# A hybrid decoder layer: the low parts of 20 weight blocks and the decay masks computed by VectorE, the last output group in halves, and a new instruction order

## The chip, the cores and the metric

The kernel runs on one core of a Trainium2 chip. The metric is the device time of one execution in microseconds (us); where several executions are given, their median. The engines are named as the profile names them: PE is the matrix engine (TensorE) and PEld its weight loads, DVE is VectorE, ACT is ScalarE, POOL is GpSimd, SP is SyncE, which in this kernel only issues DMAs. Each engine works through its own instructions in program order and waits on semaphores for the others.

## The reference

One decoder layer on a sequence of 1024 positions with a width of 1024, all in float32. The input is normalised and modulated by a vector `c`, projected to 3080 columns, and goes through two mixers: a gated linear recurrence (LRU, 4 blocks of 128 channels) and a gated delta rule in chunks (GDN, 4 heads of 128). An output projection, a residual and a squared-ReLU MLP with 4096 hidden columns follow.

```python
h = rms_norm(x, norm_mix_w[l]) * (1.0 + sc1) + sh1
proj = h @ w_in[l]
...
qkv = jax.nn.silu(causal_depthwise_conv(proj[..., o_q:o_v_end], gdn_conv_w[l]))
...
# in the delta rule, per chunk (g is summed along the chunk):
decay = jnp.exp(jnp.where(causal, g[..., :, None] - g[..., None, :], -jnp.inf))
Lmat = jnp.where(strict, jnp.einsum('bhnid,bhnjd->bhnij', k_beta, k) * decay, 0.0)
tmat = Lmat + jnp.eye(C, dtype=jnp.float32)
u = lax.linalg.triangular_solve(tmat, v_beta, left_side=True, lower=True, unit_diagonal=True)
...
attn = jnp.where(causal, jnp.einsum('bhnid,bhnjd->bhnij', q, k) * decay, 0.0)
...
mix = jnp.concatenate([out_lru, out_gdn], axis=-1) @ w_out[l]
x = x + g1 * mix
h = rms_norm(x, norm_mlp_w[l]) * (1.0 + sc2) + sh2
x = x + g2 * (jnp.square(jax.nn.relu(h @ w_up[l])) @ w_down[l])
return rms_norm(x, final_norm_w)
```

## The kernel before

**Products in split precision.** The large matrix products are made with a fast matmul type of reduced precision (`fp32r`). Each operand is split into a high part, which is the value rounded to that type, and a low part, which is what the rounding left out; a product is three matmuls (high x high, high x low, low x high). So each weight block needs a high part (a copy by ACT) and a low part. For the 20 projection blocks of 128 columns that are not keys (`z`, `q`, `v` of four heads, `lx` and `ly` of four blocks) the method `split` of `Proj` (L817) makes the low part in two steps: ACT writes the negated high part into `w_l` (L821), and a DMA on POOL's queue adds the raw weights to it while it writes (L822; the helper `Adder`, L553, gives the DMA the option to accumulate). Each such block is then used by 72 matmuls of 342 columns, in three thirds of the sequence.

**The stages.** First `x` is loaded, normalised, transposed and split, and the key projections run as their data arrive. Then follow the gate columns (`ab`), from which the cumulated decays `gcs` come; they are transposed and written to a small array in DRAM, `gdr`, so that a row of it can be spread over all partitions. For each of four heads `decay` (L1081) makes the mask of 128 x 1024: SP fills `dm` with `neg` (0 on and above the diagonal of each 128 x 128 block, -1e30 below), a DMA on POOL's queue adds the broadcast row of `gdr` to it, and ACT takes the exponential in eight pieces, with the negated decay of the row as bias. `key` (L1102) multiplies the key products `kk` by the mask into `LT`. After the fourth head `inverse` (L1135) inverts all triangular blocks: a substitution of 62 short DVE instructions for blocks of 32, then many small matmuls (`it`, `iy`, `iw`, `iz`). Beside this run the projections `z`, `q`, `v`, `lx`, `ly`, and behind them the chain of the delta rule (`ch`, `cho`) and the LRU. The output projection (`wg`, `wl`), the second norm (`h2`), and the MLP follow; the MLP's two products are made with Strassen's scheme of seven block products each (`up`: `upx`, `upy`, `upz`; down: `dn`).

**The end.** The seven block products of the down projection are summed in PSUM banks. In the last one (`at == 4`) the four output groups `j` are finished one after another, each with 24 matmuls of 512 columns, and each followed by `final_late` (L1739): gate, residual, sum of squares, the power -0.5 on POOL, the scaling by ACT and DVE in halves, and the store.

**What sets the order.** The program is not issued as it is written. `Recorder` notes each operation with its engine, its buffers and a length (L239, `Proxy.length` L496); `schedule` (L291) then simulates all engines with these lengths, with latencies between engines, a model of the matrix engine's clock (`Clock`, L201) and of the port that DVE and POOL share, and takes at each step the ready operation of the highest priority. A priority comes from the latest start that the end allows, moved by a number for each operation from the table `SHIFTS` (L246), which is packed into the source as text. The main sequence of large products keeps its written order on PE; other PE operations are put between them. Operations in a group of small matmuls (`mms`) have the lengths `L1_DUR` and `L2_DUR` and a share of activity for the clock model (L1168, L1176, L1187, L1191). The result is one fixed order for each engine and one fixed placing of buffers. All recorded operations are issued from one line, 458, so the profile shows them under L458 (small groups under L636) and they are told apart by their tiles.

Of the kernel before, what the change touches and what calls it, by code (L numbers as in the profile page):

```python
# [13 lines left out]
F32 = mybir.dt.float32  # L14
# [8 lines left out]
P = 128  # L23
# [24 lines left out]
FILL, WARM, AB_DUR, GATE_DUR, L1_DUR, L2_DUR = 1e6, 36, 0.85, 0.89, 0.066, 0.11  # L48
# [5 lines left out]
T_INIT, SP_ISSUE, SP_LAT, SP_LAND, LANES = 0.75, 0.45, 1.6, 1.0, 8  # L54
RESERVE = {"b": 11, "ps": 2, "u": 1, "c": 2}
# [67 lines left out]
def dram_box(ap):  # L123
# [7 lines left out]
    'c-p;NXLuFW+Fg523J^*Fkw{enNbe{hpdd<9svy|#N)fDx6csKYQj{W15Cpv_AVsAJ77(O}6hS)DTOb04KoU|<+3Q;;&-e4r`JTy-Z}O1jWM<Fa``znZY'  # L131
    'rT7hQlTPPg9Rv$k|{^fz*)i`=+4Dl!Z*0rEHkZn%wEQJ+{QZn{yxSrIhYb$7knRcL)G{}aCab<Q}LAXu_h{*6QNa1$a*2oa4bjI#$1^7V%FOk<1@S6c{'
    'Ka!>@is-a&oigWSz-Q&-pWVQ(l9>wY<1M_0Yj!1>Zk`k3)~yF6k=?++piG<LsW)XE4a_<o@ezna2^K(YG^$v-zU=nOC?P_0hmK&FY8`@jk|+OiR6C8>A'
    '0+sv-N<5FSkFf)O^3y)yprS+f&Y@NZK-d%1ZR-!eU_q-lW4xeJ_O&NVaK>6q6dYJPMrv~wPcS?mAMc?(B4FMU7uuthK?YKIeNYUK^G^-&b_@OMrf-#T+'
    'cF&KqhzK9t-mOIQ;3v~*XFz1ko;Vg!(T*~sMv}wabEMr=j8GMl=@jQy-3YVBD&8=K^s(*b(fJscwYKI~CgNeE8oPXtBW*r3B&%EHDfVmipuD%UOF_+Op'
    'tFz3vh>6a-ScW;iCrqpvYszb6M}19vKj3lyea=Om_wVulWR3)WG;{F~m-y4nYbfuF@xA5ja>m;BXvK`&L^B$R&Kf3~@!VjJn{mPG<}d#Q7UQX4W7I<xJ'
    'cSCuXf(+FDOk%+=V&goNyxO5SvB-guxg-hC<=S+4f7Z$+cw<8ZoxdX*QZbX_pv4iVLoSvz{l|n%5y6oRLdq<%NLky9<>>v4?@?1lNlE*%+vf%t6T(C`4'
    'Ml0e#@@S#`Xs5A=U2ADdm3^2W>5szyULqt#BIW%yj&LF?hr_x4YTV#KY(83k>1b&~iI2>-DrZLuJ#8-|3zakM7wY2fqtE!4a7?*f)46l$d$luCZOR?(p'
    'GUla?7=7ixF=Uw9<<01GiEm=fB@5Ffn#y6uP#IU6`ExG!+ZpPc>ctq%TWd9|~5220u`J{7DPIGeq|Hp+P~EAGzoIsLMi=9S4v;?3Z#+y4r+$xaP4$-6&'
    'rJ9Iv0h23G7*^8RlpIi|9jMo0n<^GRs4Lj2g3iY;qb;jHAuICoZt=AUsdG6x@{C^*>*z%bFf6i=OC=nmqiNUhUv`2U}G%r*OEzyUKur3(GVfZN+3I*)J'  # L140
    'U|0KDXsNwm?!y<MGWZ>jb7QD0hTC}M^vl5>!DL%kcWcF6xDf1S8?h|T@w#2aE}>Sop?Kg+KBkqah1s|O2QY2zc|L%Jh&PSU0820lwJ``g%nsWb)wvgIb'
    '4%N1JnFxiX@X<3yJv6m3u&S8f#}@lf_?4rP>3I}rr&afKK*R71MdXZ=j_j&mBZXVtQJ@q*u(pSD??TMPXy2Ko$Sm0l&tzW0iMV{mwh@=FSj~A45bGC3S'
    'J3#jcQ(SVK6tih~F?4+w%tax7cv5R<`fuX6J3str7Ufza>~PnCGvAQAlH!9cx>oJ7)7HH!^{L*-rL0#@kz=6lGCm<)&XhcLu9rH}6F;%(I{HTics)_%|'
    '~(!vUUgwv;z*ede$iOQS2|Fr8aD0hv4#tf8pX4VDVt9ZU$s1~*^;&oL*oPaKiXmzlyH7>^d%0E(~b;s^f9=R%jPVH>UXM0`hb4F=;`Byl@htMw}NFv;`'
    'yYGMkj!}8yJ*LfSYu!xt<;!u5i)PKz1Kd?J6E?@(*1M>q@IFbA95uW6e?624iL0i7X<Lrjf%oeU*;|a@9hJDpuW=Ce5h3t)ioN7-9xp`8QSMq1Ii7B=i'
    '%jsOYc>)376;lZ>Iw5XwTH_LXiA_sKU1S<3N7uo2Ucr}94@IqzQd;TEK3+2KMHh-)$z&!+E%a51=@eZ&x>eMECYUFq?u+UYz20}-SI@U6>K9*ObC)mRv'
    '=E1v#wzovNpqU`YB~LJN~$>%tGP=$pUN5LL-VH@jNZsG4=NIa%s|9RaR%Wb#r_ra#}q6yBYc;AUpc!`C8`~k*fUtcvmEWjI?a4>Sj-Z5++5}v+mVNDNp'
    '!|E?qDi!+uCLtcPf(x;fBydej$7w$1NJ(hqlVDakiq<!uO-Eoo_jedBJzy@w1O{eD#IXQYII_@&sF%M{&{a!y~9~p22eI+7|qV%eEA{;TJs5F8CBvQPT'
# [78 lines left out]
class Recorder:  # L227
# [63 lines left out]
    def schedule(self):  # L291
# [37 lines left out]
        while done < len(ops):  # L329
# [68 lines left out]
            if e == "SP":  # L398
# [1482 lines left out]
```

## Time and profile before

| | us |
|---|---|
| median of 3 runs | 1159.14 |
| lowest, highest run | 1156.08, 1170.63 |
| the profiled execution, device time | 1170.07 |
| its span, first to last instruction | 1168.3 |
| PE busy in the span | 1145.5 |
| DVE busy | 800.1 |
| ACT busy | 630.6 |
| POOL busy | 288.1 |

The profile is of one execution, and its 1170.07 us are near the highest of the runs shown. Busy times are sums over the span; the ends of matmuls are modelled, so a busy PE is not PE at its peak. "Idle before, releaser" tells what ended an engine's idle time. A row of a stage gives its start and end, its length, the busy time and the number of instructions of PE, PEld, DVE, ACT and POOL, the clock granted to PE (1.00 is full speed), the busy share of the DMA engines, and GB/s.

### The profile page before, as it was taken

Reading aid. Unit: us, or ns where it says so; the run is one execution under the profiler, and the core shown is the slowest. Engines: PE = TensorE matmul, PEld = TensorE weight load, DVE = VectorE, ACT = ScalarE, POOL = GpSimd, SP = SyncE. Lnnn points to the kernel's source line nnn. Section 1 sums busy time; section 2 is a strip of 40 time slices with the busy share of each in tenths; the row PEclk is TensorE's granted clock in tenths of the full one; section 3 lists DMA queues with packets and bytes.
Section 4 is the critical chain, followed back from the end, with each engine's and each line's share of the span. In section 5 each row is a group of like instructions: output and inputs, shape, how many; then the busy total and the mean of one; then the engine's idle time right before and its main releaser. Section 6 shows DMA issues by size and latency. Waiting matters only on the chain.

```text
span 1168.3 us, 16601 instructions
## 1 busy us (share of the span) xinstructions
PE 1145.5 (98%) x6264; PEld 978.9 (84%) x6264; DVE 800.1 (68%) x1114; ACT 630.6 (54%) x979; POOL 288.1 (25%) x185
## 2 busy tenths in 40 slices
PE   8999799999999999999999999999999999999997
PEld 5889798999999987778888888888788888888885
DVE  3568577578885778678867777866786386774673
ACT  4736634355548988376755555455755234442541
POOL 1103110012211433200002302331115177722140
PEclk9999898799999999999999999999999999999999
DMA  9428974366775562413187776687999976776342
GB/s 344 165 70 238 306 218 145 89 195 184 234 207 165 145 236 88 144 73 109 54 282 249 269 229 224 243 283 244 357 405 348 342 263 206 252 242 208 126 172 80
DMA packets 133298, 246.35 MB, mean 211 GB/s; under 512 B 11169, under 2 KB 54366, under 8 KB 133218
## 3 DMA queue, kind: packets, MB, share of 16 engines
q1 hardware_dynamic: 129762, 232.71, 57.8%
q0 software_dynamic: 3456, 12.58, 5.8%
q8 instruction: 49, 0.80, 0.3%
q14 instruction: 31, 0.25, 0.1%
HBM read 173.93 MB, written 58.74 MB: 199 GB/s over the span
## 4 chain that ended last, share of the span: by engine, by line
PE 91%; ACT 3%; DMA 2%; issue 2%; POOL 1%; DVE 1%; SPq 0%; POOLq 0%; ACTq 0%
PE dn L458 26%; PE upx L458 15%; PE upz L458 8%; PE q_p L458 4%; PE k_p L458 4%; PE v_p L458 4%; PE upy L458 4%; PE wl L458 4%; PE lx_p L458 3%; PE ly_p L458 3%; PE z_p L458 3%; PE wg L458 2%; PE ch L458 2%; DMA k_dm<-gdr 1%; PE cho L458 1%
## 5 line engine op out<-in xcount | busy, mean ns | idle before, releaser
L458 PE MATMUL upx<-h2h,U 128*128 128x512 f32 x512 | 168.0, 394 | 0.0
L458 POOL TENSOR_TENSOR wd<-wd,wd 128x512 f32<-128x512 f32 x32 | 52.4, 1639 | 286.8 <-DMA wd<-in_w_down_dram 176.7
L458 PEld LDWEIGHTS upx<-h2h,U 128*128 128x128 f32 x512 | 96.1, 188 | 22.8 <-issue 0.2
L458 DVE TENSOR_TENSOR U<-wu,U 128x512 fp32r<-128x512 f32 x112 | 86.7, 783 | 35.1 <-ACT U L458 34.4
L458 PE MATMUL upx<-h2l,U 128*128 128x512 f32 x256 | 100.9, 394 | 0.0
L458 ACT ACTIVATE act<-act 128x512 f32<-128x512 f32 x112 | 69.5, 631 | 39.6 <-DVE act L458 37.5
L458 PE MATMUL upz<-h2h,U 128*128 128x512 f32 x256 | 84.9, 394 | 0.0
L458 ACT CAST U<-wu 128x512 fp32r<-128x512 f32 x112 | 67.0, 616 | 26.5 <-DVE wu L458 8.4
L458 PEld LDWEIGHTS upx<-h2l,U 128*128 128x128 f32 x256 | 48.1, 188 | 11.3
L458 PEld LDWEIGHTS upz<-h2h,U 128*128 128x128 f32 x256 | 48.1, 188 | 11.3
L458 PE MATMUL upz<-h2l,U 128*128 128x512 f32 x128 | 50.4, 394 | 0.0
L458 ACT COPY ek<-upx 128x512 f32<-128x512 f32 x48 | 28.1, 585 | 36.0 <-PE upx L458 35.8
L458 DVE TENSOR_TENSOR act<-upz,ek 128x512 f32<-128x512 f32 x32 | 21.9, 688 | 34.0 <-PE upz L458 30.3
L458 PE MATMUL upy<-h2h,U 128*128 128x512 f32 x128 | 42.6, 394 | 0.0
L458 DVE TENSOR_TENSOR wu<-wu,wu 128x512 f32<-128x512 f32 x48 | 39.6, 839 | 0.6 <-DMA wu<-in_w_up_dram 0.5
L458 ACT ACTIVATE vn<-ch,bcoef 128x128 f32<-128x128 f32 x32 | 11.7, 367 | 39.8 <-PE ch L458 39.6
L458 PE MATMUL q_p<-hl,q_wh 128*128 128x342 f32 x96 | 33.0, 344 | 0.0
L458 PE MATMUL q_p<-hh,q_wh 128*128 128x342 f32 x96 | 32.8, 342 | 0.0
L458 PE MATMUL q_p<-hh,q_wl 128*128 128x342 f32 x96 | 32.4, 338 | 0.0
L458 POOL TENSOR_TENSOR ssq<-ssq,mhalf 128x1 f32<-128x1 f32 x16 | 12.1, 759 | 82.0 <-DVE ssq L458 81.9
L458 PE MATMUL z_p<-hh,z_wh 128*128 128x342 f32 x96 | 31.8, 331 | 0.0
L458 PE MATMUL v_p<-hh,v_wl 128*128 128x342 f32 x96 | 31.7, 331 | 0.0
(582 smaller groups left out, 3620.8 us busy)
## 6 DMA issues: line engine op xcount, KB each, us to landing
L<-aod SPq DMA_DIRECT2D x56, 512.0 KB, 6.4
R<-in_w_down_dram SPq DMA_DIRECT2D x40, 512.0 KB, 4.8
wu<-in_w_up_dram SPq DMA_DIRECT2D x32, 512.0 KB, 6.4
aod<-as SPq DMA_DIRECT2D x64, 256.0 KB, 3.8
wd<-in_w_down_dram SPq DMA_DIRECT2D x32, 512.0 KB
aod<-act SPq DMA_DIRECT2D x48, 256.0 KB, 2.8
x<-in_x_dram SPq DMA_DIRECT2D x16, 512.0 KB, 5.7
sc_w<-in_w_mod_dram SPq DMA_DIRECT2D x16, 512.0 KB, 5.5
```

Source lines behind the costliest of these rows:

```text
L458: op.fn(*[res(v) for v in op.a], **{n: res(v) for n, v in op.k.items()})
```

## The change

- `split`: the low part is one DVE subtraction, raw weights minus high part. ACT's negated copy and the accumulating DMA are gone, in all 20 blocks.
- `decay`: SP loads the broadcast row of `gdr` straight into `dm`, and DVE adds `neg` to it. The fill with `neg` by SP and the accumulating DMA on POOL are gone, in all four heads.
- The last output group (`at == 4`, `j == 3`) is made in two halves of 256 columns: the first half in its old PSUM bank, the second in a bank of its own (`dn4b`), while the part of the second half that lies in the old bank is added to the residual before. `final_parts` replaces `final_late` for this group and takes the sums of squares of the two halves one after the other.
- The model behind the order: the lengths and activity shares of the small matmuls, and `OVER`, by which the next instruction of DVE, ACT and POOL may start before the last one's result is there.
- The table `SHIFTS` is replaced as a whole, so the order of all instructions is new. The helper `Adder` remains in the source and is no longer used.

```diff
-FILL, WARM, AB_DUR, GATE_DUR, L1_DUR, L2_DUR = 1e6, 36, 0.85, 0.89, 0.066, 0.11
+FILL, WARM, AB_DUR, GATE_DUR, L1_DUR, L2_DUR = 1e6, 36, 0.85, 0.89, 0.07, 0.14
...
+OVER = {"DVE": 0.08, "ACT": 0.10, "POOL": 0.03}
...
 _SHIFTS = (
...
                 t = max(t, port) if op.port else t
-                now[e] = fin = t + (clock.run(t, op.dur, op.work) if e == "PE" else op.dur)
-                port = max(port, fin) if op.port else port
+                fin = t + (clock.run(t, op.dur, op.work) if e == "PE" else op.dur)
+                now[e] = fin - OVER.get(e, 0.0)
+                port = max(port, now[e]) if op.port else port
...
             A.copy(self.w[0], raw)
-            A.mul(self.w[1], self.w[0].bitcast(F32), -1.0)
-            GD.dma_start(out=self.w[1].bitcast(F32), in_=raw)
+            V.tensor_tensor(out=self.w[1], in0=raw, in1=self.w[0].bitcast(F32), op=ALU.subtract)
...
         dm = big(f"k{h}_dm")
-        SP.dma_start(out=v3(dm), in_=neg[:, None, :].to_broadcast([P, 8, P]))
-        GD.dma_start(out=dm, in_=gdr[h:h + 1, :].to_broadcast([P, T]))
+        SP.dma_start(out=dm, in_=gdr[h:h + 1, :].to_broadcast([P, T]))
+        V.tensor_tensor(out=v3(dm), in0=v3(dm), in1=neg[:, None, :].to_broadcast([P, 8, P]), op=ALU.add)
...
-                mms(L1_DUR, [(p[blk[b + 1], c], LT[blk[b], i, blk[b + 1]], xnc[blk[b], i, :], True, True) for b in (0, 2)], 0.25)
+                mms(L1_DUR, [(p[blk[b + 1], c], LT[blk[b], i, blk[b + 1]], xnc[blk[b], i, :], True, True) for b in (0, 2)], 0.2)
...
-                mms(L2_DUR, [(p[up, 64 * q:64 * q + 64], LT[lo, 8 * h + q, up], w[lo, q, :], True, True)], 0.5)
+                mms(L2_DUR, [(p[up, 64 * q:64 * q + 64], LT[lo, 8 * h + q, up], w[lo, q, :], True, True)], 0.25)
...
+    def final_parts(t, i, pa, pb, ops, v_):
+        j, e, s = fin[t], halves[1 - i], halves[i]
+        sq, rr, r = big(f"fsq{t}"), small("ssq3", 2), ssq2[:, t:t + 1]
+        for n, (p, c) in enumerate(((pa, halves_[0]), (pb, halves_[1]))):
+            xs_ = x1[t][:, s][:, c]
+            products(4, ops, (t % 4,), n == 1, True, c, p)
+            V.tensor_tensor(out=v_[:, c], in0=p[:, c], in1=g2b[:, s][:, c], op=ALU.mult)
+            V.tensor_tensor(out=xs_, in0=xs_, in1=v_[:, c], op=ALU.add)
+            A.activation(sq[:, c], xs_, AF.Square, accum_out=rr[:, n:n + 1])
+            V.scalar_tensor_tensor(out=r if n else sq2[:, t:t + 1], in0=rr[:, n:n + 1], scalar=1.0 / D, in1=sq2[:, t:t + 1],
+                                   op0=ALU.mult, op1=ALU.add)
+        rsqrt8(r, r)
+        A.mul(j[:, e], j[:, e], r)
+        V.scalar_tensor_tensor(out=j[:, s], in0=x1[t][:, s], scalar=r, in1=fnw[:, s], op0=ALU.mult, op1=ALU.mult)
+        for h in (e, s):
+            SP.dma_start(out=os_[t][:, h], in_=j[:, h])
...
         for j in range(4):
+            if at == 4 and j == 3:
+                t_, v_ = big("t4b")[:, lo_], big("t43")[:, lo_]
+                scaled(bank[3], 0, t_)
+                V.tensor_tensor(out=x1[7][:, halves_[1]], in0=x1[7][:, halves_[1]], in1=t_[:, halves_[1]], op=ALU.add)
+                rec.bias = -4.0 * j
+                final_parts(7, 0, bank[3], ps("dn4b"), ops, v_)
+                rec.bias = 0.0
+                continue
```

More of the change, by code (lines that the diff above doesn't have):

```diff
@@ L135 @@
[L135 to L144, printed above, removed]
@@ L197 @@
+    'w2<@%VMcRhoRvD#ZdUgr{9>NavcQG6;1{TckdH?lICNzJdhjoj$P9$26bSDBXsTVEFc2w^>c<AA{PUJ=%(tIJ*B6T#nD$6~VrSMjK68m(vUF|*AuQv@G'
+    'kCQQbBB%4h0rt^lWDCN~fDmZomw+pvoJsBl*{~RgYFQuU8a(JB2*!{*UtRSBM8kQq?KiVfO8!gs*&D0NU`-O6&xpe3mv<hrHgDuTwjES9AV<MIzjA!tu'
+    'vaPCeeJ1BKU(Wx8D(5zr)@vC@`}>Vb(rC3%+BCa0Pkek#VEYx=f)7k{T*)einr46C{Z+<K*o{SI5O=dLBKBi64*ZOU_}2V_vw`jIbXGYN(AxbgyB0o>!'
+    'oI-&11&?(tp'
 )
@@ L1783, in hybrid_body, with products @@
     bank = {}
-    def products(at, ops, js, first, last):
+    def products(at, ops, js, first, last, part=None, p=None):
         rec.bb = True
@@ L1789, in products @@
             cs = halves[n % 2]
+            rs = cs if part is None else slice(cs.start + part.start, cs.start + part.stop)
             for j in js:
                 ts_ = slice(cs.start + j * P, cs.start + (j + 1) * P)
-                mm3(bank[j], (l[0][:, ts_], l[1][:, ts_]), (r[0][:, cs], r[1][:, cs]), first and n == 0,
+                o = bank[j] if part is None else (p or bank[j])[:, part]
+                mm3(o, (l[0][:, ts_], l[1][:, ts_]), (r[0][:, rs], r[1][:, rs]), first and n == 0,
                     last and n == 2 * len(ops) - 1, skip_group_check=True)
```

123 lines of the change are left out of this document (65 added, 58 removed).

## The prediction

> **What bounds the kernel now.** I read the page first, then the busy time by stage, then the waits of TensorE, then the chain around the largest of them. On the page:
>
> ```profile
> span 1168.3 us, 16601 instructions
> PE 1145.5 (98%) x6264; PEld 978.9 (84%) x6264; DVE 800.1 (68%) x1114; ACT 630.6 (54%) x979; POOL 288.1 (25%) x185
> PEclk9999898799999999999999999999999999999999
> ```
>
> TensorE is busy 98% of the span; its idle time is 22.8 us in all. No edit of the other engines can win more than that, apart from time that TensorE spends at a lower clock (PEclk shows tenths and hides it). By stage (start and end in us, length, busy time of each engine, granted clock, DMA share, GB/s):
>
> ```profile
> 0.00:60.00 60.00, 56.37 (x321) 42.37 (x322) 26.74 (x62) 34.38 (x53) 7.12 (x18) 0.97 0.70 249
> 116.00:140.00 24.00, 15.84 (x96) 15.25 (x95) 12.06 (x24) 16.58 (x48) 3.84 (x5) 0.87 1.04 282
> 136.00:141.00 5.00, 5.00 (x21) 5.00 (x21) 3.66 (x8) 3.47 (x9) 1.64 (x1) 0.54 1.05 366
> 140.00:404.00 264.00, 264.00 (x2102) 257.23 (x2101) 193.79 (x304) 151.78 (x221) 48.66 (x35) 0.95 0.65 184
> 195.00:219.00 24.00, 24.00 (x176) 20.91 (x174) 10.69 (x17) 7.62 (x12) 3.22 (x2) 0.50 0.42 111
> 404.00:540.00 136.00, 132.62 (x653) 110.07 (x652) 100.04 (x149) 95.75 (x152) 36.16 (x23) 0.99 0.40 140
> 540.00:849.00 309.00, 309.00 (x1338) 249.79 (x1337) 225.83 (x306) 176.10 (x299) 55.38 (x37) 1.00 0.67 233
> 849.00:1161.00 312.00, 311.63 (x1344) 251.84 (x1342) 198.67 (x164) 128.25 (x157) 126.95 (x62) 1.00 0.68 243
> ```
>
> From 540 to 1161 us TensorE has no idle time (0.4 us) at clock 1.00: no new order can shorten these 621 us, except after their end. What can move lies before 540: 3.6 us idle in 0 to 60, 8.2 in 116 to 140, 3.4 in 404 to 540, and two stretches at half clock. The waits of TensorE from 100 to 540 us (total, times, longest):
>
> ```profile
> PE ktok L458 <- DVE LT L458: 8.1, 2, 5.9
> PE wg L458 <- POOL gcl L458: 1.3, 1, 1.3
> ```
>
> The one wait that matters is for DVE's `LT`, the masked key products. The chain that leads there (start, length, what):
>
> ```profile
> 104.69 4.94 DMA gdr<-gT
> 110.19 1.75 POOL k_dm L458 x2
> 116.24 15.20 DMA k_dm<-gdr
> 131.46 2.16 ACT k_dm L458 x7
> 133.64 0.70 DVE LT L458
> 134.48 1.09 PE ktok L458 x4
> ```
>
> So the four decay masks are written by accumulating DMAs on POOL's queue; the last lands 15.20 us after its issue, and TensorE stands until DVE has used it.
>
> **The change, part by part.** The sum is made against the profiled execution: span 1168.3 us, 1170.07 with what lies around it, while the runs shown have a median of 1159.14 and a top of 1170.63. It is thus one of the long ones.
>
> *1. Decay masks.* Four fills with `neg` on SP and four accumulations on POOL go; four plain loads of `gdr` on SP, which now wait for `gdr`, and four DVE adds come. Rows for the transfers (KB, median us to landing) and for a DVE operation of two SBUF operands with 1024 elements (mean ns):
>
> ```profile
> k_dm<-neg SPq DMA_DIRECT2D x4, 512.0 KB, 4.7
> k_dm<-gdr POOLq DMA_DIRECT2D x4, 512.0 KB, 10.3
> gcm<-catd SPq DMA_DIRECT2D x4, 512.0 KB, 3.1
> z_wl<-z_w POOLq DMA_DIRECT2D x4, 512.0 KB, 12.7
> L458 DVE TENSOR_TENSOR h2l<-h2r,h2h 128x1024 fp32r<-128x1024 f32 x8 | 9.7, 1219 | 0.0
> ```
>
> `gdr` lands at 109.6 us (104.69 + 4.94). No row shows this load alone: it lies between 3.1 us (`gcm`, plain) and 15.2 (the slowest accumulation); I take 4.7, the plain transfer of the same size to the same tile. The second to fourth come behind it: 2.1 MB in all, at the 282 GB/s of the window 116 to 140 some 7.4 us, so the last lands at about 118, not 131.4. Each mask then costs DVE 1.22 us and ACT its eight exponentials, some 2.5 us as now (2.16 us for seven). ACT works through four masks in 10 us and ends near 126, the last `LT` near 127 instead of 138. TensorE's 8.1 us of waiting goes, and with it the half-clock stretch right behind it: 136 to 141 has clock 0.54, so 5 us x 0.46 = 2.3 us were lost there, and the four `ktok` transposes (1.09 us) and the key products before it ran slow as well; I take 3.0. What is late next? DVE is busy 12.06 of the 24 us there, so 4.9 us of adds fit; TensorE has z projections to run, which themselves waited for accumulating DMAs (12.7 us median for `z_wl`) and no longer do. If that cover is missing, up to 8.1 us stay. The new wait stands at the head of the DVE queue: behind an add that waits for its load stand the key convolutions, `ssk` and `ktail`, and TensorE's `ktok` banks wait for these. On SP the load waits for `gdr` as POOL does now:
>
> ```profile
> 110.19 1.75 POOL L458 DMA_DIRECT2D k_dm<-gdr  x2 [10.59 <-DMA gdr<-gT]
> 107.44 0.32 SPq L458 DMA_DIRECT2D kd<-ktail  x1
> 113.28 0.32 SPq L458 DMA_DIRECT2D zd<-z_st  x1
> ```
>
> SP issues nothing from 107.8 to 113.3 us, so at that place the wait holds nobody up; placed earlier, it would hold the later loads by at most the 4.94 us of `gdr`. I take 0 and keep 5 as the upper end.
>
> *2. Low parts of 20 weight blocks.* ACT loses 20 negations, POOL 20 issues, the DMA queues 20 transfers; DVE gains 20 subtractions.
>
> ```profile
> L458 ACT ACTIVATE z_wl<-z_wh x4: 1045/1050/1062, 82.6 to 115.4; 128x1024 fp32r<-128x1024 f32 x4
> 84.00:116.00 32.00, 32.00 (x236) 31.32 (x235) 27.09 (x65) 19.50 (x31) 9.39 (x7) 1.00 0.87 225
> DVE LT L458 <- PE iz L636: 9.7, 2, 7.3
> DVE S L458 <- PE ch L458: 15.7, 13, 2.6
> 161.40 11.32 PE q_p L458 x72
> ```
>
> ACT gets back 20 x 1.05 = 21 us, DVE pays 20 x 1.22 = 24.4, with the masks 29.3. From 140 to 404 DVE has 193.79 us of 264; with the 16 subtractions of the later blocks it has 213, so it stays under TensorE, which is always busy there. Between 84 and 116 it is fuller: 27.09 of 32, and 29.5 with the two subtractions whose products run there. From the count of busy time the cost is 0. Against it stands the order: DVE works in program order, and a subtraction placed behind an operation that waits for TensorE (7.3 us at `iz`, 2.6 at `ch`) is late for the next projection. Bounds: -1.3 us (the wait of `wg`, which freed time on ACT and POOL may close) to the third rival below. I take 0, the nearer end by the busy times: one projection gives TensorE 11.32 us (the `q_p` row), and the 1.22 us of the next one's subtraction can lie anywhere beside it.
>
> [...]
>
> ```profile
> L458 DVE TENSOR_TENSOR R_5l<-R,R_5h 128x1024 fp32r<-128x1024 f32 x8 | 18.8, 2345 | 10.3 <-ACT R_5h L458 4.3 <-POOL xb L458 3.7 <-POOL R L458 2.3
> 956.00:984.00 28.00, 28.00 (x123) 22.63 (x122) 21.26 (x11) 10.35 (x14) 21.82 (x10) 1.00 0.66 223
> ```
>
> The same subtraction takes 2345 ns on average where POOL is busy 21.82 of 28 us. POOL in 140 to 404 is busy 48.66 of 264, a good part of it the issues that go, so at most every fifth of the 24 meets it: 5 x 1.1 us = 6 us on DVE, which has room. [...]
>
> *3. Last output group in two halves.* The final 24 matmuls of 512 columns become 48 of 256.
>
> ```profile
> 58.93 11.66 PE k_p L458 x95
> 848.85 306.21 PE dn L458 x1320
> 1160.67 0.69 DVE L458 TENSOR_TENSOR t<-dn,g_bc 128x512 f32<-128x512 f32 x1 [1.74 <-PE dn L458]
> 1161.40 0.69 DVE L458 TENSOR_TENSOR xb<-xb,t 128x512 f32<-128x512 f32 x1
> 1162.12 0.63 ACT L458 ACTIVATE fsq<-xb 128x512 f32<-128x512 f32 x1 [3.22 <-DVE xb L458]
> L458 DVE TENSOR_TENSOR h2l<-h2r,h2h 128x256 fp32r<-128x256 f32 x24 | 9.6, 419 | 0.3
> ```
>
> Matmuls of 256 to 258 columns come every 11.66 / 95 = 0.123 us, those of 512 every 306.21 / 1320 = 0.232: 48 x 0.123 - 24 x 0.232 = +0.3 us. Behind the last matmul two DVE operations shrink from 0.69 to about 0.42 and ACT's square from 0.63 to about 0.4: -0.8. The first half's own operations lie under the second half's 2.9 us of matmuls. Net -0.5 us. Between nothing and -1.
>
> *4. The new order.* It changes no work. Its lengths for small matmuls and its overlap of successive operations only place things. What it can touch is the second half-clock stretch: 195 to 219 at 0.50 while the inverse of the triangular blocks runs: 24 us in which 12 were lost. 1170.07 - 12 = 1158 lies between the other two runs shown (1156.08, 1159.14), and 1170.63 - 12 = 1158.6 too: I read it as a stretch that some executions have. In the sum it goes: -12. [...]
>
> **Sum:** 1170.1 - 8.1 - 3.0 - 0.5 - 12 = 1146.5, and from the median 1159.1 - 11.6 = 1147.5. I forecast **1147 us**.
>
> **The rivals.**
> *The half clock returns* in the typical run, by 195 to 219 or another stretch in the inverse: 1147 + 12 = 1159. For: one profile has it, and a run of 1170.63; the small products stay as small. Against: two of three runs shown seem without it.
> *It doesn't do what it says:* the masks are still late, since the DMA engines are full (share 1.04 in 116 to 140) and DVE takes them late; the wait only changes its name: 1147 + 8 + 3 = 1158.
> *Slower: TensorE waits for subtractions.* One mechanism: a low part sits on DVE behind an operation that waits for TensorE, and the projection stands at its `w_l`. For: DVE has such waits (7.3 us at `iz`, thirteen at `ch` with 15.7 in total) in the very stretch. Price: 20 blocks x 1.5 us, about the mean at `ch` (15.7 / 13 = 1.2) and more at `iz`, is 30: 1177; with half-clock windows behind the stalls 1185. It decides from 12 / 20 = 0.6 us per block, where all that was won is gone.
> *Much faster:* the order also closes the 3.6 and 3.4 us of idle time and the partial clock in 404 to 540 (0.01 x 136 = 1.4): 1147 - 8 = 1139; under 1136 only with still more of the start.
>
> **How the numbers follow.** Forecast 0.50 (1141 to 1153), half clock 0.17 (1155 to 1164), wait renamed 0.15 (1153 to 1163), slower 0.13 (1160 to 1188), much faster 0.05. The range 1138 to 1168 leaves out most of the slower case and half of the much faster one, and some edges: 2 in 10. Two per cent of 1159.14 is 23 us, about what a measurement of this kernel can tell from no change: faster means under 1136 (0.04), slower over 1182 (0.06), within 0.90.
>
> **What would show it.** Right: TensorE without idle time between 110 and 140 us, no wait for `LT` over 1 us, no accumulating DMA; `k_dm` on SP landing in under 8 us; DVE at 80 to 85% in 140 to 404 with TensorE always busy; the end some 7 us behind the last matmul instead of 7.7. Wrong: a wait of TensorE for a `w_l` of DVE in the projections, clock under 1.00 between 150 and 230, or a first stage (0 to 60) that the new order has made longer; I have costed the last at 0 because the same loads, 249 GB/s there, carry it.

## The result

The changed kernel is slower: 1171.52 us (median of 20 runs, 1167.13 to 1175.92) against 1159.55 (20 runs, 1156.08 to 1170.96), a ratio of 1.008 with a 95% interval of 1.0054 to 1.0107. The forecast was 1147. The difference is under 2%, but the interval excludes a gain and even a draw.

Executions of before are of two kinds, about two of three at 1156 to 1161 us and one of three at 1167 to 1171, and since the profile that the prediction read was of the second kind, the experiments begin with a trace of the first (`e0`).

The profile page of after: busy times and granted clock.

```profile
span 1165.8 us, 16532 instructions
...
PE 1139.4 (98%) x6288; PEld 974.9 (84%) x6288; DVE 839.0 (72%) x1143; ACT 613.5 (53%) x961; POOL 275.1 (24%) x161
...
PEclk9999998999999998999999999999999999999999
```

TensorE is idle for 26.4 us (1165.8 - 1139.4), where before it was 22.8. By stage (columns as in the prediction's table):

```profile
116.00:140.00 24.00, 24.00 (x167) 23.98 (x167) 19.71 (x38) 18.53 (x39) 5.82 (x3) 1.00 1.01 377
140.00:220.00 80.00, 75.46 (x820) 71.83 (x819) 65.06 (x119) 26.81 (x43) 3.93 (x3) 0.91 0.35 113
140.00:404.00 264.00, 257.40 (x2090) 250.24 (x2089) 217.72 (x315) 137.29 (x199) 37.32 (x18) 0.97 0.43 138
179.00:183.00 4.00, 4.00 (x39) 3.18 (x29) 3.87 (x5) 3.30 (x5) 0.00 (x0) 0.57 0.81 248
196.00:207.00 11.00, 11.00 (x59) 9.99 (x60) 3.35 (x7) 2.65 (x4) 0.00 (x0) 0.53 0.17 53
404.00:540.00 136.00, 127.70 (x599) 103.44 (x598) 100.43 (x147) 87.34 (x143) 34.74 (x22) 0.97 0.37 132
```

From 116 to 140 us TensorE is now busy all 24 us at full clock, as forecast. But from 140 to 404 it is idle for 6.6 us and has clock 0.97, where before had no idle time (and clock 0.95 in the profile that the prediction read, 1.00 in `e0`), and from 404 to 540 it is idle 8.3 us instead of 3.4. Two stretches in the inverse have half the clock. The new waits of TensorE (total, times, longest):

```profile
PE lrus L461 <- POOL msum L461: 3.8, 1, 3.8
PE ch L461 <- DVE nv L461: 3.0, 1, 3.0
PE h2T L461 <- ACT h2r L461: 2.9, 7, 0.7
...
PE h2T L461 <- DVE h2r L461: 1.7, 3, 0.7
...
PE it L639 <- DVE xnc L461: 0.9, 1, 0.9
```

No wait for `LT` is left. In its place stand waits of the substitution (`xnc`), of the chunk loop (`nv`), of the LRU's end (`msum`) and of the second norm (ten for `h2r`, 4.6 us).

When each stage starts shows where the lead goes. The view of single tiles gives for a form of matmul the count, the shortest, middle and longest duration in ns, and the first and the last start in us; here of `e0`, then of after:

```profile
L458 PE MATMUL q_p<-hh,q_wh x96: 313/318/423, 161.2 to 283.1; 128*128 128x342 f32 x96
...
L458 PE MATMUL lx_p<-hh,lx_wh x96: 312/319/404, 302.7 to 407.0; 128*128 128x342 f32 x96
...
L458 PE MATMUL wg<-wo4h,gch x16: 389/395/776, 418.8 to 467.4; 128*128 128x512 f32 x16
...
L458 PE MATMUL upx<-h2h,U x512: 387/394/481, 524.6 to 835.2; 128*128 128x512 f32 x171
```

```profile
L461 PE MATMUL q_p<-hh,q_wh x96: 313/320/492, 148.4 to 282.0; 128*128 128x342 f32 x96
...
L461 PE MATMUL lx_p<-hh,lx_wh x96: 313/319/408, 299.7 to 405.0; 128*128 128x342 f32 x96
...
L461 PE MATMUL wg<-wo4h,gch x16: 389/396/775, 418.6 to 471.6; 128*128 128x512 f32 x16
...
L461 PE MATMUL upx<-h2h,U x512: 386/394/405, 529.7 to 843.3; 128*128 128x512 f32 x171
```

After reaches the first q projection 12.8 us ahead (148.4 against 161.2), the first LRU projection only 3.0 ahead, the output projection `wg` 0.2 ahead, and the MLP (`upx`) 5.1 behind. The same reading for the kernels of the experiments, each number being the time from the first matmul of a stage to the first matmul of the next, in us:

```
stage            e0     after  e1     e3     e4     h1     x2     y5
start to q_p     161.2  148.4  160.1  160.4  151.0  148.2  152.0  149.4
q_p to lx_p      141.5  151.3  141.6  145.4  148.1  147.6  151.0  144.6
lx_p to wg       116.1  118.9  116.2  119.7  119.4  119.6  119.4  116.1
wg to upx        105.8  111.1  104.2  104.0  111.6  103.8  103.5  104.4
upx to dn        313.6  316.6  313.8  313.7  320.0  313.7  313.6  313.7
dn to the end    319.6  319.5  319.4  319.0  318.8  319.8  319.6  319.5
span             1157.8 1165.8 1155.3 1162.2 1168.9 1152.7 1159.1 1147.7
```

After against `e0`: -12.8, +9.8, +2.8, +5.3, +3.0, -0.1, together +8.0. (The profiled execution of after, 1167.61, is one of its quicker ones; the median lies 3.9 higher.) So the question for the experiments is what costs 9.8 us from the first q projection to the first LRU projection, the stage with the triangular inverse, and 8.3 us from `wg` to `dn`.

### The profile page after: what moved, and what is told of

Read it like the earlier page. It is cut to its first block, busy times and chain, and to the rows that moved or that the text cites. A ratio compares the mean times of both kernels' runs of the same rounds, so it can differ in the third digit from the quotient of the medians.

```text
span 1165.8 us, 16532 instructions
## 1 busy us (share of the span) xinstructions
PE 1139.4 (98%) x6288; PEld 974.9 (84%) x6288; DVE 839.0 (72%) x1143; ACT 613.5 (53%) x961; POOL 275.1 (24%) x161
## 4 chain that ended last, share of the span: by engine, by line
PE 78%; DVE 11%; ACT 6%; issue 2%; POOL 1%; DMA 1%; SPq 0%; POOLq 0%; ACTq 0%; DVEq 0%
PE dn L461 26%; PE upx L461 14%; PE upz L461 7%; PE k_p L461 4%; PE upy L461 4%; PE q_p L461 3%; PE v_p L461 3%; PE wl L461 3%; PE lx_p L461 2%; PE ch L461 2%; PE ly_p L461 2%; PE cho L461 1%; PE wg L461 1%; ACT ta L461 1%; DVE xr L461 1%
## 5 line engine op out<-in xcount | busy, mean ns | idle before, releaser
L461 PEld LDWEIGHTS upx<-h2l,U 128*128 128x128 f32 x256 | 48.1, 188 | 11.4 <-issue 0.2
L461 PEld LDWEIGHTS upz<-h2h,U 128*128 128x128 f32 x256 | 48.1, 188 | 11.1
L461 DVE TENSOR_TENSOR wu<-wu,wu 128x512 f32<-128x512 f32 x48 | 36.9, 774 | 1.4 <-DMA wu<-in_w_up_dram 1.2
L461 POOL TENSOR_TENSOR fin<-xb,fnw 128x512 f32<-128x512 f32 x11 | 22.2, 2023 | 45.1 <-DVE xb L461 26.9
L461 PE MATMUL v_p<-hh,v_wh 128*128 128x342 f32 x96 | 31.9, 333 | 0.0
L461 POOL TENSOR_TENSOR R<-R,R_5o 128x1024 f32<-128x1024 f32 x8 | 23.1, 2887 | 37.1 <-DMA R_5o<-in_w_down_dram 37.1
```

Source lines behind the costliest of these rows:

```text
L461: op.fn(*[res(v) for v in op.a], **{n: res(v) for n, v in op.k.items()})
```

## The experiments

To part the edits from the order, the edits were put into before's order: what an instruction does is replaced (`rec.ops[-1].fn` is the operation noted last), and its place kept. Later the two orders were spliced: every engine follows the one order up to a given matmul, and the other from there. Kernels of one group ran beside the same runs of before (medians 1159.36, 1160.61, 1159.91, 1159.39, 1159.84, 1159.70).

### Is the wait for `LT` there in a quicker execution of before? (e0)

Before, unchanged.

> Before, unchanged, for a trace of an execution without the long stretch at half clock, if it gives one (about two of three did). If the 8.1 us wait for LT belongs to every execution: the wait is there again, 7 us or more, and the time is about 1158. If it belongs to the long execution that was profiled: under 4 us of it at 1158.

Measured: 1159.62. Its waits for `LT`, and two stretches:

```profile
PE ktok L458 <- DVE LT L458: 5.6, 2, 3.3
```

```profile
120.00:130.00 10.00, 6.65 (x30) 6.46 (x31) 4.24 (x8) 6.35 (x18) 0.21 (x1) 0.66 1.03 250
140.00:220.00 80.00, 80.00 (x872) 76.76 (x872) 63.67 (x120) 37.26 (x59) 10.13 (x9) 1.00 0.66 201
```

The wait is 5.6 us here instead of 8.1, between the two expectations, with a clock of 0.66 around it. From 140 to 220 us the clock is 1.00 and TensorE always busy: the long stretch of the first profile belongs to some executions only.

### The edits in before's order (e1, e2, e3), and after without its subtractions (e4)

`e1`, masks:

```diff
         SP.dma_start(out=v3(dm), in_=neg[:, None, :].to_broadcast([P, 8, P]))
+        rec.ops[-1].fn = lambda **k: None
         GD.dma_start(out=dm, in_=gdr[h:h + 1, :].to_broadcast([P, T]))
+        rec.ops[-1].fn = lambda out, in_, accum_op: nc.sync.dma_start(out=out, in_=in_)
...
+                    nc.vector.tensor_tensor(out=d.real(), in0=d.real(), op=ALU.add,
+                                            in1=neg[:, None, :].to_broadcast([P, 8, P]).real())
```

> The order of before is kept, instruction for instruction; only the four decay masks change: no fill with neg, a plain load of gdr where the accumulating DMA was issued, and one DVE add ahead of each mask's first exponential. All theories: the wait of TensorE for LT (8.1 us) goes. My prediction's step 1 alone, 8.1 + 3.0 = 11.1 us: about 1146 to 1148 beside a before of 1157 to 1159. Rival (the inverse simply falls into a low clock once it comes earlier): a stretch of 10 us or more at clock 0.5 between 170 and 220 us in the trace, and a time of 1153 to 1160.

`e2`, low parts:

```diff
             A.mul(self.w[1], self.w[0].bitcast(F32), -1.0)
+            rec.ops[-1].fn = lambda *a, **k: None
             GD.dma_start(out=self.w[1].bitcast(F32), in_=raw)
+            h, l = self.w[0].bitcast(F32), self.w[1]
+            rec.ops[-1].fn = lambda out, in_, accum_op: nc.vector.tensor_tensor(out=l.real(), in0=in_, in1=h.real(),
+                                                                                op=ALU.subtract)
```

> The order of before is kept; only the 20 low parts change: no negation on ACT, and where POOL issued the accumulating DMA, DVE subtracts. Theory 'the added DVE load makes DVE late for TensorE in any order': 1165 or more beside a before of 1157 to 1159. Theory 'the new order loses it': no change, 1155 to 1160, as step 2 of the prediction has it (0, and up to -1.3).

`e3` has both.

> Both edits of e1 and e2 in the order of before; of the change only the new order and the halved last group are missing. Theory 'the new order loses it': about 1146 to 1148, so more than 20 us faster than after. Theory 'the added DVE load': 1160 or more. Theory 'low clock in the inverse, whatever the order': 1153 to 1165 with 10 us or more at clock 0.5 between 170 and 220 us.

`e4` leaves the low part out; the matmuls read the high part in its place:

```diff
             V.tensor_tensor(out=self.w[1], in0=raw, in1=self.w[0].bitcast(F32), op=ALU.subtract)
+            h, l = self.w[0], self.w[1]
+            def skip(out, in0, in1, op):
+                l.buf.tile = h.buf.get()
+            rec.ops[-1].fn = skip
```

> After, in its own order, with the 20 subtractions left out: the matmuls that read a low part read the high part of the same block in its place (the same number of matmuls of the same shape; the result is less exact or wrong, and no low part is made). Theory 'DVE load': the time falls by 15 us or more, to 1147 to 1155. Theory 'the new order itself': within 5 us of after, 1163 to 1171, with the same late nv of DVE and the same stretches at half clock in the trace.

Measured, medians: e1 1163.26 (ratio 1.0024, interval 0.9987 to 1.0061; six executions at 1157.1 to 1158.5 and six at 1168.0 to 1168.7, so the median stands between), e2 1163.11 (1.0019, 0.9987 to 1.0051; eleven of twelve at 1161.3 to 1165.0), e3 1164.82 (1.0055, 1.0024 to 1.0087), e4 1169.92 (1.0068, 1.0032 to 1.0104).

`e1` and `e3` miss what my theory expected, and `e3` lies where the theory of the DVE load had it. `e4` bears my theory out: in after's order the subtractions are worth 1.6 us by the medians, which the intervals don't resolve (its trace has 3.2 less from `q_p` to `lx_p` and gives them back elsewhere), so the DVE load isn't what makes after slow. `e1` wins little, since the wait is still there. The waits of `e1`, then its DVE and ACT around the first mask in order of time (start, length, what, and in brackets the idle time before it):

```profile
PE ktok L458 <- DVE LT L458: 3.8, 2, 3.0
PE kk L458 <- DVE LT L458: 2.7, 1, 2.7
```

```profile
119.20 1.22 DVE L1094 TENSOR_TENSOR k_dm<-k_dm,neg 128x1024 f32<-128x1024 f32 x1
122.34 0.69 DVE L458 TENSOR_TENSOR LT<-kk,k_dm 128x512 f32<-128x512 f32 x1 [1.93 <-ACT k_dm L1096]
...
120.45 2.15 ACT L1096 ACTIVATE k_dm<-k_dm,ngc 128x128 f32<-128x128 f32 x7 [2.56 <-DVE k_dm L1094]
```

The load lands early enough (SP issues the first two from 109.48 us, the median landing is 4.6 us later, and DVE doesn't wait ahead of the add at 119.20), but the add stands behind the key convolutions, right ahead of the exponentials, and add, exponentials and `LT` follow one another while TensorE waits 6.5 us. And against `e1`, `e3` shows what the subtractions cost in before's order: its executions without the long stretch take 1163.8 to 1165.7, those of `e1` 1157.1 to 1158.5, some 7 us less. `e2` agrees: 4 to 5 us over before's own quicker executions, between what the two theories had. The table has 3.8 of the 7 from `q_p` to `lx_p` and 3.5 from `lx_p` to `wg`. No trace shows TensorE waiting for a low part of the 20 blocks; it waits for what stands behind the subtractions on DVE, in `e3` for these:

```profile
PE it L636 <- DVE xnc L458: 1.6, 1, 1.6
PE ch L458 <- DVE r L458: 1.5, 2, 1.2
```

### Where the add must stand (h4)

`e1` with each add earlier on DVE, by the two traces 1 to 6 instructions. The order around the first two adds, without what lies further on:

```diff
-DVE: ... k3T, bcoef, ssk, bcoef, ncoef, z_b, k3T, add, LT, add, ...
+DVE: ... k3T, add, bcoef, ssk, bcoef, ncoef, z_b, k3T, add, LT, ...
```

> As e1 (before's order, masks by plain load and DVE add, low parts by DMAs), but each of the four adds stands 2 to 7 DVE instructions earlier, where its load has landed. In e1 TensorE still waited 6.5 us for LT, since each add stood right ahead of the exponentials, behind convolutions. Theory 'the masks' 8.1 us can be won, by where the add stands': wait for LT under 2 us and 1148 to 1153 in the quicker of its executions (e1 1157). Rival 'the wait is renamed': 1156 to 1158.

Measured: 1164.54 (ratio 0.9965, 0.9925 to 1.0005); four executions at 1153.2 to 1154.0, eight at 1163.9 to 1166.4. The wait for `LT` is 2.7 us (1.4 and 1.3), not under 2, and the quicker executions are 4 us below those of `e1`: part of the masks' time can be won by the place of the add. The first q projection starts at 156.8 us, 4.4 ahead of `e0` (`e1`: 160.1, 1.1 ahead). The long stretch at half clock (191 to 215 us here) is in most executions now, by the times in eight of twelve.

### Splicing the two orders (h1, h2, h5, x2)

In all of these the edit is in what the planner hands out (`splice` goes through a fixed list, `ORDER`):

```diff
-        for i in self.schedule():
+        for i in self.splice():
```

`h1`: after's order to the first q projection, then before's.

> All edits of the change but the halved last group. Each engine follows the order of after up to the first matmul of the first q projection (148 us in after), and from there the order of before. Reckoned by TensorE's lost time (what its matmuls took over their usual distance): by 140 us after has lost 18 us, before's order with the same edits (e3) 31; from 140 on e3 loses 31, after 48. Theory 'the new order wins 13 us at the start and gives it back in the inverse and behind 300 us': 1165 - 13 = 1152 (1149 to 1156). Rival 'whoever comes early to the inverse loses it there, in whatever order': 1158 to 1165, with half clock between 165 and 215 us.

`h2`: before's order to the second LRU projection, then after's.

> All edits, the halved last group too. Order of before up to the first matmul of the second LRU projection (about 320 us), from there the order of after. Theory 'the new order loses some 12 us of its own between 300 and 560 us, at the LRU's end and the second norm': 1165 + 12 = 1177 (1173 to 1180), with a wait of TensorE for msum over 3 us and half clock behind it. Rival 'that loss is only what was late from before 300 us': 1162 to 1167.

`h5`: after's order to the second LRU projection, then before's.

> All edits but the halved last group; order of after up to the first matmul of the second LRU projection (some 320 us), from there the order of before. In after TensorE loses 26.5 us from 300 us on, in h1 17.4. Theory 'the rest of the loss lies in the inverse, 140 to 220 us': about 1171 - 9 = 1162 (1158 to 1164), and 5 to 8 above h1. Rival 'the inverse of after costs nothing by itself': as h1, 1155.

`x2`: after's order to the first `lrus` matmul, then before's.

> All edits but the halved last group; order of after up to the first lrus matmul (458 us), from there the order of before on all engines. Theory 'the order of the LRU's end and the second norm itself loses 9 to 10 us there': 1161 to 1164. Rival 'what is late there was late before': 1168 to 1172.

Measured: h1 1155.35 (ratio 0.9946, 0.9905 to 0.9988), h2 1189.94 (1.0205, 1.0155 to 1.0254), h5 1167.32 (1.0040, 1.0006 to 1.0074), x2 1160.09 (0.9983, 0.9951 to 1.0014).

`x2` is the cleanest: every engine follows after's order up to the first `lrus` matmul, and it is 11.4 us faster, though it lacks the halved last group. What after loses behind that point is thus the order of the last part itself, not lateness from before it. The two stages (start and end, length, busy times, clock), in after and in `x2`:

```profile
440.00:480.00 40.00, 36.23 (x151) 29.18 (x150) 28.60 (x33) 14.03 (x19) 16.96 (x9) 0.91 0.27 93
480.00:545.00 65.00, 60.47 (x287) 47.90 (x286) 44.96 (x99) 44.07 (x91) 4.79 (x8) 1.00 0.30 106
```

```profile
196.00:210.00 14.00, 12.68 (x65) 11.20 (x66) 5.64 (x10) 3.02 (x5) 0.00 (x0) 0.51 0.27 93
440.00:480.00 40.00, 38.20 (x172) 30.66 (x171) 33.16 (x33) 15.16 (x20) 18.56 (x9) 1.00 0.35 118
480.00:545.00 65.00, 63.55 (x306) 51.62 (x305) 50.58 (x107) 45.54 (x95) 4.92 (x8) 1.00 0.30 106
```

In after TensorE is idle 3.8 + 4.5 us and loses 3.6 to the clock (40 x 0.09); in `x2` it is idle 1.8 + 1.5 and loses nothing. `h1` shows the other end: after's order up to the first q projection is worth 1164.82 - 1155.35 = 9.5 us against `e3`. `h2` and `h5` missed their numbers, and their seams are to blame at least in part: `h2` has a new wait of 6.3 us (`cho` for `vn`) and half clock from 368 to 376, `h5` one of 3.0 (`sh_c` for `sh_acc`) and half clock from 346 to 357. (The profile of `h2` is of its longest execution, which has 24 us at half clock in the inverse as well.) Beyond that they settle nothing.

### Is it the early `lrus`? (x1)

Before has the matmuls `lrus` behind the first half of `wg7`, after behind `wg5`. `x1` moves them back and changes nothing else; its order, by blocks:

```diff
-PE: ... wg50 wg51 lrus wg60 wg61 wg70 wg71 ...
+PE: ... wg50 wg51 wg60 wg61 wg70 lrus wg71 ...
```

> After, all instructions and their order kept, but the 16 matmuls lrus (sums for the LRU's norm) move on TensorE from behind block wg5 to behind the first half of wg7, where before has them. Theory 'the new order sends TensorE to lrus before POOL has msum': the wait of 3.8 us and the half clock behind it (6.8 us at 0.50, 3.4 lost) go: 7 less than after, 1163 to 1166. Rival 'msum is late whatever TensorE does, and its user stands later instead (wl, the second norm)': 1168 to 1172.

Measured: 1170.89 (ratio 1.0065, 1.0029 to 1.0102), 0.6 below after and in the rival's range. Its waits and the two stages:

```profile
PE upy L588 <- DVE U L588: 3.4, 2, 2.8
PE wl L588 <- POOL lcl L588: 3.1, 2, 2.2
PE h2T L588 <- ACT h2r L588: 2.9, 7, 0.7
...
PE h2T L588 <- DVE h2r L588: 1.6, 3, 0.7
```

```profile
440.00:480.00 40.00, 36.92 (x167) 29.61 (x166) 33.72 (x38) 15.10 (x21) 19.21 (x10) 1.00 0.32 105
480.00:545.00 65.00, 59.93 (x283) 47.14 (x281) 44.96 (x99) 43.95 (x90) 4.74 (x8) 1.00 0.29 102
```

The wait for `msum` and the half clock behind it go (clock 1.00 from 440 to 480), and 3.1 us for `lcl` come. From `wg` to `upx` this takes 107.2 us, 3.9 less than after. From `upx` to `dn` it takes 321.8, 5.2 more, with 3.4 us of waiting for `U` and half clock from 694.7 to 698.1. That second loss need not come from the move: `e4`, in after's own order, waits 3.1 us for `U` and takes 320.0 there, while the profiled execution of after, one of its quicker ones, waits 0.6. The seven plus three waits for `h2r` are what they were. So the move wins in its own stage and nothing in the median, and `lrus` alone isn't at fault; which instructions of the other engines would have to move with it was not tried.

### Subtractions in a serial chain (h3, h7)

`h3` is `h1` with the 13 low parts behind the cut made as before; in `h7` those of v0 and q1 are made so too. In `h1` and `h3` these two stand inside the substitution, and the inverse waits for that chain. DVE of `h1`, and its wait:

```profile
149.24 1.22 DVE L587 TENSOR_TENSOR v_wl<-v_w,v_wh 128x1024 fp32r<-128x1024 f32 x1
...
151.63 1.22 DVE L587 TENSOR_TENSOR q_wl<-q_w,q_wh 128x1024 fp32r<-128x1024 f32 x1
...
164.91 2.09 DVE L587 STREAM_TRANSPOSE xnc<-xx 128x1024 f32<-128x1024 f32 x1
```

```profile
PE it L765 <- DVE xnc L587: 3.0, 1, 3.0
```

The edit, here of `h7` (`h3` has the list without v0 and q1; the negations are issued at their places of before):

```diff
             V.tensor_tensor(out=self.w[1], in0=raw, in1=self.w[0].bitcast(F32), op=ALU.subtract)
+            if self.name in ('v0', 'q1', 'v1', 'q2', 'v2', 'q3', 'v3', 'lx0', 'ly0', 'lx1', 'ly1', 'lx2', 'ly2', 'lx3', 'ly3'):
+                h, l = self.w[0].bitcast(F32), self.w[1]
+                rec.negs[len(rec.ops) - 1] = lambda: nc.scalar.mul(l.real(), h.real(), -1.0)
+                rec.ops[-1].fn = lambda out, in0, in1, op: nc.gpsimd.dma_start(out=l.bitcast(F32).real(), in_=in0, accum_op=ALU.add)
```

> As h1, but the 13 low parts that are made behind the cut (v1, q2 and on) are made as before, by a negation on ACT and an accumulating DMA from POOL, at the places of before. Theory 'the subtractions in before's order cost some 6 us (e3 against e1)': h1 - 5, about 1147 (1144 to 1151). Rival 'the place decides, not the means': as h1 within 2 us.

> As h3 (after's order up to the first q projection, then before's; 13 low parts behind the cut by accumulating DMAs), but the low parts of v0 and q1 are made by DMAs too: in h1 and h3 these two subtractions stand on DVE inside the serial chain of the substitution (62 short operations, each needing the one ahead), and TensorE waits 3.0 and 2.9 us for xnc, which that chain makes. Theory 'a subtraction inside a serial chain delays its end by its whole length': the wait for xnc goes, and 1150 to 1153 in the median (h3 1156). Rival 'the chain has room, the wait comes from elsewhere': wait and time as h3.

Measured: h3 1156.29 (ratio 0.9945, 0.9904 to 0.9987; single executions from 1148.95 to 1165.27), h7 1160.18 (0.9970, 0.9932 to 1.0008). The median of `h3` misses the 1147 of my theory and is within 1 us of `h1`, as its rival had it; four of its twelve executions lie at 1149 to 1152.8, and the profiled one, 1161.12, has half clock from 186 to 210. From `h3` to `h7` the wait for `xnc` falls from 2.9 to 1.1 us, most of the 2 x 1.22 us of the two, and the quickest execution of `h7` is at 1147.18. But nine of its twelve lie at 1160 to 1161.5, so the median misses what I expected. The windows of `h7` show the stretch again:

```profile
169.00:184.00 15.00, 14.69 (x361) 13.45 (x361) 14.39 (x17) 9.43 (x15) 0.00 (x0) 1.00 0.46 143
184.00:208.00 24.00, 24.00 (x181) 20.83 (x176) 10.05 (x16) 7.49 (x11) 3.23 (x2) 0.50 0.43 129
```

TensorE is never idle from 184 to 208 us by this profile (the ends of matmuls are modelled) and has half its clock all the time. Just ahead of that it ran 361 mostly small matmuls in 15 us. Of the 181 in the stretch 100 are of 64x64 and 42 of 32x32; 21 are wide ones (128x342), at most seven in a row (197.10 to 199.39). In the next row of them, from 205.47 on, the duration of one falls from 0.49 to 0.32 us at 208, when the clock is full again.

### What decides the clock in the inverse (y1 to y4)

`h7` with more work for TensorE: matmuls of 128x512 on operands that lie there, into the bank that the next group overwrites. They change no result.

```diff
-    def mms(dur, items, share=1.0):
+    def mms(dur, items, share=1.0, fill=None):
         def several():
+            while fill:
+                w_ = hT[0][0].real()
+                nc.tensor.matmul(fill.pop().real(), w_[:, 0:P], w_[:, 0:512], start=True, stop=True, skip_group_check=True)
```

`y1` has one ahead of each of the 12 groups, `y2` two, `y3` two ahead of the four groups of the first level alone, `y4` one ahead of the eight groups of the second.

> As h7, with one more matmul of 128x512 (fp32r, its result overwritten at once) ahead of each of the 12 groups of small matmuls of the inverse: 12 x 0.23 = 2.8 us more work. h7 had executions of two kinds, 1147 to 1152 and 1160 to 1162, 9 of 12 of the second, with 24 us at half clock in the inverse. Theory 'too little large work in the inverse lets the clock fall': the second kind gets rare, and the median falls to 1150 to 1153 in spite of the 2.8 us. Rival 'only the moment decides': the same two kinds, each 2.8 us later, median 1163.

> As y1 with two such matmuls ahead of each group, 24 x 0.23 = 5.5 us more work. Theory 'too little large work': no execution with 24 us at half clock, all between 1152 and 1157. Rival 'only the moment decides': two kinds, 1153 to 1157 and 1165 to 1167, the second in most.

> As y1, but the added matmuls (128x512, results overwritten) stand only ahead of the 4 groups of the first level of the inverse (it, iy: 320 matmuls of 32 columns within some 8 us), two each: 8 x 0.23 = 1.8 us. y1 (12, one ahead of every group) had 8 of 12 executions at 1152 to 1156. Theory 'the clock falls for what the first level does': most at 1149 to 1154. Rival 'the second level (iw, iz, 64 columns) decides': most as h7's long ones, 2 later, 1160 to 1163.

> As y1, but the added matmuls stand only ahead of the 8 groups of the second level (iw, iz), one each: 1.8 us. Theory 'the second level decides': most at 1149 to 1154. Theory 'the first level decides': most at 1160 to 1163. If both y3 and y4 lie between, with half their executions long, it is the sum of the work that counts.

Measured: y1 1155.26 (ratio 0.9964, 0.9926 to 1.0002; 8 of 12 at 1152.5 to 1155.8, the other four from 1160.3 up), y2 1159.11 (1.0002, 0.9971 to 1.0033), y3 1151.37 (0.9897, 0.9855 to 0.9940; 1150.2 to 1152.0), y4 1153.88 (0.9965, 0.9923 to 1.0007; 7 of 12 at 1151.6 to 1153.9). Adding 2.8 us of work makes the kernel 4.9 us faster than `h7`, and 1.8 us at the right place 8.8 us faster. `y3`, and `y5` below with the same inverse, have no long execution in 18; `y4`, with the same added time, has five in 12. So the place of the added matmuls counts: ahead of the first level, 320 matmuls of 32 columns, the eight are worth most. `y2`, which has the same eight there and 16 more at the second level, meets neither theory: its quicker executions are 7 us above those of `y3`, though the 16 are 3.7 us of work, and five of its twelve lie at 1161.5 to 1165.8, without a trace. The same part of the inverse in `y3`:

```profile
166.00:208.00 42.00, 41.46 (x617) 37.07 (x617) 32.12 (x40) 20.21 (x31) 3.25 (x2) 1.00 0.48 139
```

By what rule the clock is granted, no run shows. In the row of `h7` TensorE is busy 24.00 of 24.00 us at 0.50, so in that stretch being busy didn't bring the full clock. That these eight wide matmuls keep the clock in the inverse is shown by the times and by the row of `y3` (clock 1.00 from 166 to 208); whether small ones of the same total length would do it too was not tried, and why more of them are not better stays open.

### The halved last group alone, and the best version (y5)

```diff
-            if False:
+            if at == 4 and j == 3:
...
                 final_parts(7, 0, bank[3], ps("dn4b"), ops, v_)
```

> As y3, with the last output group in two halves as after has it; nothing else differs. Step 3 of the prediction: -0.5 us (between 0 and -1), so about 1150.9 beside y3's 1151.4, and the end of the trace some 7 us behind its last matmul where y3 has 8. If the halves cost what 48 short matmuls cost over 24 long ones and win nothing behind: 1151.7.

Measured: 1150.94 (ratio to before 0.9903, 0.9867 to 0.9938; 1149.6 to 1154.7), 0.4 below `y3`, which this spread doesn't resolve. The last matmul and the last operation ahead of the output's DMA, in order of time, in `y5` and then in `y3`:

```profile
1140.24 0.28 PE L588 MATMUL dn4b<-R_4h,L_4l 128*128 128x256 f32 x1
...
1142.84 0.75 DVE L588 SCALAR_TENSOR_TENSOR fin<-xb,ssq,fnw 128x512 f32<-128x512 f32 x1 [0.66 <-POOL ssq L588]
```

```profile
1141.46 0.39 PE L587 MATMUL dn<-R_4h,L_4l 128*128 128x512 f32 x1
...
1144.91 0.75 DVE L587 SCALAR_TENSOR_TENSOR fin<-xb,ssq,fnw 128x512 f32<-128x512 f32 x1 [0.66 <-POOL ssq L587]
```

From the start of the last matmul to the end of the span `y5` takes 1147.7 - 1140.24 = 7.5 us and `y3` 1149.8 - 1141.46 = 8.3. From the first `dn` matmul to the end the table has 319.5 for `y5`; `y3` takes 1149.8 - 830.2 = 319.6. So 0.9 us are won behind the last matmul and 0.8 paid before it. Only 0.2 of these are the halved group's: its 48 matmuls take 5.57 us from the first start to the last (1134.67 to 1140.24), the 24 of `y3` 5.33 (1136.13 to 1141.46). The other 0.6 lie ahead of it, and no run shows why.

`y5` is the best version: after's order up to the first q projection, before's from there, masks by DVE, low parts of q0 and the four z blocks by DVE, the other 15 by accumulating DMAs, eight added matmuls, and the last group in halves. It beats before by 0.97% and after by 20.6 us.

## Why the prediction was wrong

*Step 1, decay masks: the wait goes, but not as the sum had it.* The load takes what I took for it (4.7); the DMA issues of after (count, KB each, median us to landing), then the last `LT` and what TensorE has begun by then:

```profile
k_dm<-gdr SPq DMA_DIRECT2D x4, 512.0 KB, 4.6
```

```profile
128.05 0.40 PE L461 MATMUL z_p<-hh,z_wh 128*128 128x342 f32 x1
...
132.31 0.68 DVE L461 TENSOR_TENSOR LT<-kk,k_dm 128x512 f32<-128x512 f32 x1
```

The last `LT` starts at 132.31, not near the 127 forecast, and only 5.7 us ahead of `e0` (138.00). TensorE doesn't wait for it because z projections run from 128.05 on: the cover that I named as a condition. The lead at the first q projection is 12.8 us for 11.1, but that the sizes agree is luck. The edit alone wins 1.1 us by then in before's order (`e1`), where 6.5 us of waiting stay, within the 8.1 that I named for a missing cover; with the adds placed better (`h4`) it wins 4.4, and 2.7 of waiting stay. The other 8.4 come with the new order, which I had costed at 0, for one by making `gT`, from which `gdr` comes, 10.2 us earlier (first row `e0`, second after):

```profile
104.34 0.27 PE L458 MATMUL gT<-ident,gcs 128*32 128x128 f32 x1
```

```profile
94.10 0.27 PE L461 MATMUL gT<-ident,gcs 128*32 128x128 f32 x1
```

*Step 2, low parts at 0: about right for after, wrong as a rule.* DVE is busy 217.72 of 264 us from 140 to 404 (82%; 80 to 85 were forecast), and leaving the subtractions out of after gives 1.6 us by the medians. But "can lie anywhere beside" the 11.32 us of a projection failed as soon as the order was held: 7 us in before's order, and two subtractions inside the substitution's chain are worth 1.8 us of waiting (`h3` against `h7`; after has the same two in the chain and waits 0.9 us for `xnc`, `e4` not at all). The slower rival named the right queue and the wrong victim: not the `w_l` of a projection, which no trace shows TensorE waiting for, but what stands behind.

*Step 3, halves: -0.5 forecast, -0.1 in the traces.* The part behind the last matmul is as forecast (-0.8; measured -0.9), and so are the matmuls (+0.3; 0.2 by their starts). The 0.6 ahead of the halved group were not in the sum, and the medians (0.4 apart) don't resolve the whole.

*Step 4, the new order: this step failed.* "It changes no work" is true, and costing it at 0 for that reason was the mistake: it wins some 8 us at the start and loses more behind. From the last part of the LRU through the second norm it costs 10.6 us by the table (after against `x2`: 7.6 from `wg` to `upx`, 3.0 behind), 11.4 by the medians. It puts `lrus` and the second norm's transposes earlier than the side engines deliver, and half clock follows the wait of `lrus` (3.6 us lost). From `q_p` to `lx_p` after costs 9.8 more than `e0`: 4.5 us of idle time from 140 to 220 (75.46 of 80 us busy, where `e0` has 80.00; 3.0 for `nv`, 0.9 for `xnc`, 0.6 for `ttc`) and two stretches at half clock. Not all of this is shown to be the order's: 6.6 of it remain in `e4`, without subtractions (148.1), and 6.1 in `h1`, with subtractions and before's order from there (147.6). How the 9.8 divide stays open.

*The 12 us at half clock.* I took them as a thing that some executions have. For before that holds, but its median lies among the executions without them, so nothing was to be won there, and 1147.5 from the median rested on the masks and halves alone. In after there are two shorter ones (179 to 183 and 196 to 207; 4 x 0.43 + 11 x 0.47 = 6.9 us lost), and `e4`, `x1` and `x2`, which share its order there, have the second of them too. The first rival named the place and had 12 us in the typical run; measured are 5 to 7 lost in every profiled execution with that order.

The sum by measured steps, against `e0`: -12.8 by the first q projection, +9.8 in the inverse, +2.8 to `wg`, +8.3 to `dn`, -0.1 at the end. The 2.8 to `wg` are there without subtractions too (`e4`, 119.4), so in after's order they are the order's. From 300 to 420 us TensorE is busy 117.94 of 120 in after, 120.00 in `e0`; the waits there are two ahead of `cho`, 0.8 for `vn` and 1.3 for nothing that the profile shows.

Open is which entries of the order make the second norm late beyond `lrus`, and whether after's own order would keep its clock with the added matmuls of `y3`.

## What to carry to other kernels

A new order of the same work is an edit with a price of its own: ask of each dependent small matmul which engine feeds it and whether that engine is ahead of it, and test edits in the old order before judging them in the new. Small work placed in a serial chain of another engine can delay its end by most of its length (1.8 of 2.4 us here, from `h3` to `h7`), though the engine has idle time on average (DVE is busy 197 of 264 us from 140 to 404 in `h3`). And where TensorE's clock falls in a stage of many tiny matmuls, a few wide ones among them can pay for themselves (eight did here, 1160.18 to 1151.37 us; 24 hardly did, 1159.11).

## What the hardware showed unexpectedly

TensorE ran at half clock for 24.0 us without one idle interval (`h7`, 184 to 208: 24.00 of 24.00 us busy, clock 0.50), and by the times it did so in some executions of one program and not in others: nine of twelve of `h7` took the 12 us longer that this costs. By the traces' clock records the stretches at half clock up to 560 us last 3.4 (after, 179 to 183), 6.8 (after, 459 to 467), 10.2 (after, 196 to 207), 13.7 (`x2`, `h5`) or 23.9 us (`h7`, 183 to 208), each within 0.1 us of a multiple of 3.4. Eight more matmuls of 128x512, 1.8 us of work whose results are thrown away, made the median 8.8 us shorter (1160.18 to 1151.37).
